# Where the scatters and transposes of a top-4-of-32 expert layer stand between the weight matmuls

## The chip, the core and the metric

The kernel runs on one NeuronCore of a Trainium2 chip. The metric is the device time of one execution in microseconds (us); the median of three runs of the kernel before is 1267.49 us (1266.92 to 1268.07). The engines are TensorE (PE, with its weight loads PEld), VectorE (DVE), ScalarE (ACT), GpSimd (POOL) and SyncE (SP), which issues the loads of the weights.

## The reference

One decoder layer on 512 tokens of 1024 numbers, all in float32: a mixing part (pooling and attention, not touched here) and then a mixture of 32 experts, of which each token takes four.

```
logits = ht @ w_router + b_router
top_vals, top_idx = lax.top_k(logits, TOP_K)
gates = jax.nn.softmax(top_vals, axis=-1)
...
gu = xblk @ w_gate_up[e] + b_gate_up[e]
gate = jnp.minimum(gu[:, :D_EXPERT], SWIGLU_LIMIT)
up = jnp.clip(gu[:, D_EXPERT:], -SWIGLU_LIMIT, SWIGLU_LIMIT)
act = gate * jax.nn.sigmoid(SWIGLU_ALPHA * gate) * (up + 1)
return act @ w_down[e] + b_down[e]
...
y = jnp.zeros((T + 1, D), h.dtype).at[row_tok].add(row_gate[:, None].astype(h.dtype) * yb)
```

After it the residual is added and a last RMSNorm is taken. Every expert's weights are read once, 12 MB each.

## The kernel before

The first 200 us hold the mixing part and the router. Then comes the loop that this change touches: 32 positions, each with one expert, ordered by how many tokens an expert has. `KINDS` says of a position whether it is small (S, up to 64 tokens) or big (B, up to 128).

A position has twelve **items**: eight of gate and up (`gu`, k = 0 to 7) and four of down (`dn`, j = 0 to 3), with 1 MB of weights each, which SP loads into a ring of slots. A big item splits its weights into a rounded part (`mhi`, by ACT, L937) and a rest (`mlo`, by DVE or POOL, L938), and multiplies three ways at full width: twelve matmuls into banks `x`. A small item multiplies in float32 with 64 columns of the array, two matmuls side by side, into banks `y`; each of its instructions shows as two rows in the profile. A planner (`interleave`) lays down once for all how the items of big positions (and of 0 and 31), called x, and those of the small ones, called y, take turns; its result `plan` is fixed and not touched. A row of small items in the plan without a big one in between is called a small block.

Around the items there is smaller work that PE also does, all of it through two PSUM banks `m`:

- `gather(r)`: two groups of four transposes that turn the rows fetched for a position (`xr`). For a big position four ACT pieces (`xgh`, L894) and four DVE pieces (`xgl`, L895) empty each group; for a small pair one DVE pass does (`xgs`, L917).
- `turn(r)`: transposes of the activation `au` (L1004 to L1008 compute it, from `ag` to `au`), emptied into `ats`, or `ath` and `atl`. There is a queue "turn x" for big positions and "turn y" for small ones.
- `arrive`: the slot sums, four short matmuls from `aux` and `oh`, and the fetch by an indirect DMA.
- `rest`: above all `combine`, the **scatter** of a finished position back to the tokens: eight times two matmuls at full width (`sc` with `ybh` and `ybl`, or `ss` with `ysh` and `ysl`), each pair followed by a DVE add into `y` (L1148).

Each of these is a generator in one of five queues, and `step` advances the first of every queue by one piece. Before, `step()` is called once behind every item, and in a big item once more in its middle (where `gate_up` and `down` yield). PE keeps the order in which the program writes it; on DVE and ACT a scheduler orders the work when the program is built. A piece of `turn` that is still waiting is taken in front of the down item that needs it.

Of the kernel before, what the change touches and what calls it, by code (L numbers as in the profile page):

```python
# [51 lines left out]
GAPX, GAPY, GAPN, GAPEND = 5, 2, 1, 3  # L52
TURN, SHORT = 0.2, 3.0
NFREE = 12
FILL1 = 2
FT = 3
FN = ((0, 1), (1, 3), (1, 3), (3, 4))
# [43 lines left out]
def mm3(pe, out, shi, slo, mhi, mlo, first, last):  # L101

    pe.matmul(out, lhsT=shi, rhs=mhi, start=first, stop=False)
    pe.matmul(out, lhsT=shi, rhs=mlo, start=False, stop=False)
    pe.matmul(out, lhsT=slo, rhs=mhi, start=False, stop=last)
# [20 lines left out]
def block_kernel(ctx: ExitStack, tc: tile.TileContext, xT, x, pos, vecs, w_in, w_pool, w_qb, w_kvb, w_out,  # L126
# [19 lines left out]
    y = cst.tile([P, NT, D], F32, name="y")  # L146
# [257 lines left out]
    for g, w in enumerate(WINDOWS):  # L404
        cur, step, lo_ = us[g], 1, 1
# [138 lines left out]
    def out_proj(z, c, tt):  # L544

        cs = slice(c * T, (c + 1) * T)
        for k in range(4):
            if ("out", z, c, k) in wraw:
                parts[z, c, k] = split_w(("out", z, c, k))
        po = {}  # L550
        for k in range(4):
            for t in tt:
                if k == 0:
                    po[t] = pt("po", bufs=5 if c and z else 7)
                ts = slice(t * P, (t + 1) * P)
                mm3(PE, po[t], mix["h", z][:, k, ts], mix["l", z][:, k, ts], *parts[z, c, k], k == 0, k == 3)
                yield
        for t in tt:
            V.scalar_tensor_tensor(y[:, t, cs], po[t], grms[z][:, t:t + 1], y[:, t, cs], op0=ALU.mult, op1=ALU.add)
# [193 lines left out]
    for t in range(NT):  # L753
        for _ in out_proj(1, 1, [t]):
            for _ in range(FILL1):
                while todo and next(todo[0], 0) == 0:
# [26 lines left out]
    def bank(tag):  # L783
        return pools["pm"].tile([P, T], F32, tag=tag, bufs={"x": 4, "y": 2, "m": 2}[tag], name=tag)
# [57 lines left out]
    onehot, slots, xg, yb, scat, actT = {}, {}, {}, {}, {}, {}  # L842

    def big(r):
        return r == "o" or KINDS[r] == "B"

    def onx(r):

        return big(r) or r == 0 or r == E - 1
# [94 lines left out]
    def split_item(r, what, k):  # L944

        w = wslots.pop((r, what, k))
        out_ = []
        for hf in range(2):
            out_.append(split(w[:, hf * D:(hf + 1) * D], G if nsplit[0] % 4 == 1 else V))
            nsplit[0] += 1  # L950
        presplit[r, what, k] = out_

    def fixed(r):
        return r != "o" and r < NFIX

    def biases(r, cs):
        for c in cs:
            bs = bias[:, c * T:(c + 1) * T]
            if big(r):
                PE.matmul(banks[r][c], lhsT=m4b[0:96, r:r + 1].to_broadcast([96, P]), rhs=bs, start=True, stop=False)  # L960
            else:
                q = 64 * (c % 2)
                PE.matmul(banks[r][c // 2][q:q + 64, :], lhsT=m4b[0:96, r:r + 1].to_broadcast([96, 64]), rhs=bs,
                          start=not fixed(r), stop=fixed(r))

    def gate_up(r, k):

        first = r == "o"
        if k == 0:
            banks[r] = [bank("x" if onx(r) else "y") for _ in range(4 if big(r) else 2)]  # L970
        if big(r):

            todo = [(hf, c) for hf in range(2) for c in range(2)] if k < KD - 1 else [
                (hf, c) for c in range(2) for hf in range(2)]
            parts = presplit.pop((r, "gu", k))
            for n, (hf, c) in enumerate(todo):
                cs = slice(c * T, (c + 1) * T)
                if k == 0 and not first:
                    biases(r, [2 * hf + c])
                mm3(PE, banks[r][2 * hf + c], xg[r][0][:, k, :], xg[r][1][:, k, :], parts[hf][0][:, cs],  # L980
                    parts[hf][1][:, cs], first and k == 0, k == KD - 1)
                if n == 1:
                    yield
        else:
            w = wslots.pop((r, "gu", k))
            for c in range(4):
                q = 64 * (c % 2)
                if k == 0 and c % 2 == 0 and not fixed(r):
                    biases(r, [c, c + 1])
                PE.matmul(banks[r][c // 2][q:q + 64, :], lhsT=xg[r][:, k, :], rhs=w[:, c * T:(c + 1) * T],  # L990
                          start=(k == 0 and fixed(r)), stop=(k == KD - 1 and not fixed(r)))

                if k == KD - 1 and c % 2 == 1 and fixed(r):
                    biases(r, [c - 1, c])
# [16 lines left out]
    def act(r):  # L1011
        b = banks.pop(r)
        return [swiglu(b[c], b[2 + c]) for c in range(2)] if big(r) else [swiglu(*b)]
# [139 lines left out]
    def spread(gf):  # L1153

        for c in range(2):
            cs = slice(c * T, (c + 1) * T)
            pb = bank("m")
            PE.matmul(pb, lhsT=ones[0:1, :], rhs=gf[0:1, cs], start=True, stop=True)
            S.copy(gf[:, cs], pb)
# [258 lines left out]
    plan = [v for b in blocks for v in b]  # L1418
# [13 lines left out]
    def later(g, n):  # L1432

        for _ in range(n):
            yield
        yield from g


    groups = {}
# [6 lines left out]
    def arrive(r):  # L1446

        for q in groups[r]:
            select(q)
            yield  # L1450
            slot_info(q)
        fetch(r)
# [3 lines left out]
    def load(what, r, k):  # L1456

        if r < NFIX and r not in wgu:
            wgu[r] = load_expert(r, r)
        if r not in wgu:  # L1460
            with tc.issue_after(lastload[-1]):
                wgu[r] = load_expert(r, nc.sync.value_load(eid[0:1, r:r + 1], min_val=0, max_val=E - 1))
        if what == "gu":
            load_gate_up(r, wgu[r], [k])
        elif r == E - 1:
            load_down_last(r, wdown[r], k)
        else:
            load_down(r, wdown[r], [k])
# [12 lines left out]
    def firsts(g):  # L1481
        return plan.index(("gu", g, 0))
# [4 lines left out]
    bigs = [r for r in range(E) if big(r)]  # L1487
# [6 lines left out]
            assert fetch_at[g] > KD, g  # L1494
    queues = {"turn x": [], "turn y": [], "gather": [], "arrive": [], "rest": []}

    def step(drain=None):

        for name, q in queues.items():
            if drain and name not in drain:  # L1500
                continue
            while q:
                if next(q[0], 0) == 0:
                    q.pop(0)
                elif not drain:
                    break
# [21 lines left out]
    for i, (what, r, k) in enumerate(plan):  # L1528

        PE.on = i >= NFREE  # L1530
        while loaded < min(i + (14 if i > 2 else 9), len(loads)):
            load(*loads[loaded])
            loaded += 1
        if big(r):
            n = xorder.index((what, r, k))
            assert n < nsp
        for g, at in fetch_at.items():
            if at == i:
                queues["arrive"].append(arrive(g))
        for g, at in turn_at.items():  # L1540
            if at == i:
                queues["gather"].append(gather(g))
        if (what, r, k) == ("gu", E - 1, 0):
            gf = mo.tile([P, D], F32, tag="xgh", bufs=1, name="gf")
            dma(gf[0:1, :], g_final)
        if k == 0 and what == "gu" and r > 0:
            assert r in xg, (r, i)
        if what == "dn" and k == 0:
            step(("turn x" if onx(r) else "turn y",))
        if what == "dn" and k == KD // 2 - 1:  # L1550

            while ("b" if big(r) else "s") in pending:
                step()
        if (what, r, k) == ("dn", E - 1, 0):
            step(queues)
            down_last(r, gf)
            break
        for _ in gate_up(r, k) if what == "gu" else down(r, k):
            step()

        ahead = n + 3 if big(r) else 2 if (what, r, k) == ("dn", 0, KD // 2 - 2) else 0
        for v in xorder[nsp:ahead]:
            split_item(v[1], v[0], v[2])
        nsp = max(nsp, min(ahead, len(xorder)))
        if what == "gu" and k == KD - 1:
            if r == E - 1:
                spread(gf)
            queues["turn x" if onx(r) else "turn y"].append(later(turn(r, act(r)), 3))
        if what == "dn" and k == KD // 2 - 1 and r < E - 2:
            if big(r):  # L1570
                queues["rest"].append(later(marked("b", combine([r])), 3))
            elif halfdone[0] is None:
                queues["rest"].append(later(marked("s", combine(["s"], r < NFIX)), 3))
        step()
    rt.close()

    PE.on = False
# [95 lines left out]
```

## Time and profile before

| what | value |
|---|---|
| median of three runs | 1267.49 us |
| profiled execution | 1268.17 us, span 1266.4 us |
| granted clock, mean over the span | 0.981 |
| PE busy | 1213.0 us (96%) |
| DVE busy | 865.4 us (68%) |
| ACT busy | 542.7 us (43%) |
| POOL busy | 303.7 us (24%) |
| HBM read | 429.71 MB, 343 GB/s over the span |
| chain that ended last | PE 74%, DVE 7% |

The span runs from the first to the last instruction of one profiled execution; 1.8 us lie around it. Busy shares are means over parts with different limits. A row of the timeline gives an instruction's start and length, and in brackets how long its engine stood idle before it and what ended that. PE rows overlap: the distance of two starts tells what one costs, not the length.

### The profile page before, as it was taken

Reading aid. Unit: us, or ns where it says so; the run is one execution under the profiler, and the core shown is the slowest. Engines: PE = TensorE matmul, PEld = TensorE weight load, DVE = VectorE, ACT = ScalarE, POOL = GpSimd, SP = SyncE. Lnnn points to the kernel's source line nnn. Section 1 sums busy time; section 2 is a strip of 40 time slices with the busy share of each in tenths; the row PEclk is TensorE's granted clock in tenths of the full one; section 3 lists DMA queues with packets and bytes.
Section 4 is the critical chain, followed back from the end, with each engine's and each line's share of the span. In section 5 each row is a group of like instructions: output and inputs, shape, how many; then the busy total and the mean of one; then the engine's idle time right before and its main releaser. Section 6 shows DMA issues by size and latency. Waiting matters only on the chain.

```text
span 1266.4 us, 16525 instructions
## 1 busy us (share of the span) xinstructions
PE 1213.0 (96%) x5597; PEld 697.3 (55%) x5597; DVE 865.4 (68%) x1552; ACT 542.7 (43%) x785; POOL 303.7 (24%) x272
## 2 busy tenths in 40 slices
PE   7979999899999998999999999999999999999994
PEld 6856674345655555555555555555645555555332
DVE  6897674657767676676768667776765876767344
ACT  6466650135525443354354435435434454444013
POOL 2355362112212121221123113221312122212001
PEclk9999999899999998999999999999999999999997
DMA  8312428999999998999998999999999999999981
GB/s 313 100 51 88 146 90 313 409 421 415 416 419 411 404 405 322 360 413 416 402 377 348 420 388 399 402 386 393 381 416 358 361 421 403 377 380 399 422 333 69
DMA packets 86849, 435.17 MB, mean 344 GB/s; under 512 B 9223, under 2 KB 9223, under 8 KB 53992
## 3 DMA queue, kind: packets, MB, share of 16 engines
q1 hardware_dynamic: 82818, 420.43, 83.4%
q0 software_dynamic: 3744, 13.24, 2.7%
q8 instruction: 45, 0.74, 0.2%
q10 hardware_dynamic: 198, 0.39, 0.1%
q14 instruction: 44, 0.36, 0.1%
HBM read 429.71 MB, written 4.33 MB: 343 GB/s over the span
## 4 chain that ended last, share of the span: by engine, by line
PE 74%; DVE 7%; DMA 1%; issue 1%; ACT 1%; POOL 0%; DVEq 0%; ACTq 0%; POOLq 0%
PE x L118 33%; PE y L118 29%; PE m L118 11%; DVE mlo L938 3%; DMA bdraw<-in_b_down_dram 1%; DVE au L1007 1%; ACT mhi L937 1%; DVE oh L859 0%; DVE au L1008 0%; DVE ag L1004 0%; DVE au L1006 0%; DVE xgl L895 0%; DVE ss L1096 0%; DVE y L1130 0%; DVE o L1186 0%
## 5 line engine op out<-in xcount | busy, mean ns | idle before, releaser
L937 ACT CAST mhi<-slot 128x1024 fp32r<-128x1024 f32 x288 | 300.6, 1049 | 260.9 <-PE x L118 236.1
L938 DVE TENSOR_TENSOR mlo<-slot,mhi 128x1024 fp32r<-128x1024 f32 x216 | 288.3, 1347 | 66.3 <-ACT mhi L937 65.8
L938 POOL TENSOR_TENSOR mlo<-slot,mhi 128x1024 fp32r<-128x1024 f32 x72 | 177.4, 2464 | 642.5 <-ACT mhi L937 642.4
L118 PE MATMUL y<-slot,xgs 128*64 128x512 f32 x1152 | 276.0, 602 | 0.0
L1148 DVE TENSOR_TENSOR y<-y,m 128x512 f32<-128x512 f32 x168 | 115.0, 684 | 121.8 <-PE m L118 121.4
L118 PE MATMUL x<-mhi,xgh 128*128 128x512 f32 x384 | 164.0, 427 | 0.0
L118 PE MATMUL x<-mlo,xgh 128*128 128x512 f32 x384 | 152.0, 396 | 0.1
L118 PE MATMUL x<-mhi,xgl 128*128 128x512 f32 x384 | 151.4, 394 | 0.0
L118 PEld LDWEIGHTS y<-slot,xgs 128*64 128x64 f32 x1152 | 76.1, 137 | 130.4 <-issue 126.9
L118 PE MATMUL y<-slot,ats 128*64 128x512 f32 x608 | 144.5, 612 | 0.7 <-ACT ats L1036 0.7
L1005 ACT ACTIVATE as<-ag 128x512 f32<-128x512 f32 x44 | 27.8, 632 | 160.7 <-DVE ag L1004 160.7
L118 PEld LDWEIGHTS x<-mhi,xgh 128*128 128x128 f32 x384 | 72.7, 189 | 25.7 <-issue 12.2
L118 PEld LDWEIGHTS x<-mhi,xgl 128*128 128x128 f32 x384 | 72.1, 188 | 17.0
L118 PEld LDWEIGHTS x<-mlo,xgh 128*128 128x128 f32 x384 | 72.4, 189 | 15.9 <-DVE mlo L938 1.1
L118 PEld LDWEIGHTS y<-slot,ats 128*64 128x64 f32 x608 | 39.7, 138 | 74.3 <-issue 70.5
L118 PE MATMUL x<-mhi,ath 128*128 128x512 f32 x192 | 64.2, 416 | 0.0
L118 PE MATMUL x<-mlo,ath 128*128 128x512 f32 x192 | 61.4, 401 | 0.0
L118 PE MATMUL x<-mhi,atl 128*128 128x512 f32 x192 | 60.9, 398 | 0.0
L1098 ACT ACTIVATE ysh<-y,sl 64x512 fp32r<-64x512 f32 x36 | 24.6, 684 | 80.4 <-PE y L118 80.1
L1100 DVE SCALAR_TENSOR_TENSOR ysl<-y,sl,ysh 64x512 fp32r<-64x512 f32 x36 | 27.0, 750 | 42.4 <-ACT ysh L1098 41.9
L881 POOL DMA_INDIRECT xr<-hrow,idx x21 | 28.7, 1367 | 94.5 <-DVE idx L878 48.7
L894 ACT ACTIVATE xgh<-m,gs 128x128 fp32r<-128x128 f32 x96 | 33.4, 366 | 31.9 <-PE m L118 16.7
(401 smaller groups left out, 1737.1 us busy)
## 6 DMA issues: line engine op xcount, KB each, us to landing
slot<-in_w_gate_up_dram SPq DMA_DIRECT2D x256, 1024.0 KB, 10.4
slot<-in_w_down_dram SPq DMA_DIRECT2D x128, 1024.0 KB, 9.9
wraw<-in_w_in_dram SPq DMA_DIRECT2D x16, 256.0 KB, 5.7
wraw<-in_w_out_dram SPq DMA_DIRECT2D x16, 256.0 KB, 2.6
xtraw<-in_xT_dram SPq DMA_DIRECT2D x8, 256.0 KB, 5.9
y<-in_x_dram SPq DMA_DIRECT2D x4, 512.0 KB, 7.3
hrow<-part POOLq DMA_DIRECT2D x8, 256.0 KB, 3.3
out_dram<-o SPq DMA_DIRECT2D x4, 512.0 KB, 2.7
```

Of the source, the lines that this page charges most:

```text
L118: r = f(*args, **kwargs)
L881: G.indirect_dma_start(out=rows[r], out_offset=None, in_=hrow, in_offset=bass.IndirectOffsetOnAxis(ap=idx[:, 0:1], axis=0), bounds_check=T ...
L894: S.activation(hi[:, d, :], v, AF.Copy, scale=g)
L937: S.copy(hi, src)
L938: eng.tensor_tensor(lo, src, hi.bitcast(F32), op=ALU.subtract)
L1005: S.activation(sg, g, AF.Sigmoid, scale=1.702)
L1007: V.scalar_tensor_tensor(u, u, 1.0, g, op0=ALU.add, op1=ALU.mult)
L1098: S.activation(yh[ps_, c], db[ps_, :], AF.Copy, scale=slots[r][ps_, 6:7])
L1100: V.scalar_tensor_tensor(yl[ps_, c], db[ps_, :], slots[r][ps_, 6:7], yh[ps_, c].bitcast(F32), op0=ALU.mult, op1=ALU.subtract)
L1148: V.tensor_tensor(y[:, t, cs], y[:, t, cs], pb, op=ALU.add)
```

## The change

`step` gets a second argument, `only`: the queues that may advance. With it:

- Behind a small item only "turn x" advances, but for the last item of a small block, behind which two full steps are taken.
- If a big position comes up within `SOON` = 4 items and its rows are not gathered yet, "gather" may advance behind a small item as well.
- In the middle of a big item every queue but `rest` advances, so no scatter stands there; behind it all do.
- Where a position's rows are still missing at its first item, the gather is driven until they are there.

```diff
+SOON = 4
...
-    def step(drain=None):
+    def step(drain=None, only=None):
 
         for name, q in queues.items():
-            if drain and name not in drain:
+            if name not in (drain or only or queues):
                 continue
...
         if k == 0 and what == "gu" and r > 0:
-            assert r in xg, (r, i)
+            while r not in xg:
+                step(only=("gather",))
...
+        beside = None if onx(r) or i < firsts(bigs[0]) else ("turn x",)
+        within = beside or ("turn x", "turn y", "gather", "arrive") if big(r) else beside
+        if beside and any(0 < firsts(g) - i <= SOON and g not in xg for g in groups if big(g)):
+            beside += ("gather",)
         for _ in gate_up(r, k) if what == "gu" else down(r, k):
-            step()
+            step(only=within)
...
-        step()
+        if beside and i + 1 < len(plan) and onx(plan[i + 1][1]):
+            for _ in range(2):
+                step()
+        else:
+            step(only=beside)
```

The plan of items, the loads and the arithmetic stay as they are. The order moves on PE, DVE and ACT; SP's is the same.

**PE, items 0 to 2 of gate and up of small position 9** (a small block between big position 6's items; `y` matmuls are the small ones, `sc` with `ybh` and `ybl` a scatter), before:

```order
L118 MATMUL y<-slot,xgs 64x512 x2
L118 MATMUL m<-ybh,sc 128x512
L118 MATMUL m<-ybl,sc 128x512
L118 MATMUL y<-slot,xgs 64x512 x4
L118 MATMUL m<-ybh,sc 128x512
L118 MATMUL m<-ybl,sc 128x512
L118 MATMUL y<-slot,xgs 64x512 x4
L118 MATMUL m<-ybh,sc 128x512
L118 MATMUL m<-ybl,sc 128x512
```

and now:

```order
L119 MATMUL y<-slot,xgs 64x512 x10
L119 MATMUL m<-ybh,sc 128x512
L119 MATMUL m<-ybl,sc 128x512
L119 MATMUL m<-ybh,sc 128x512
L119 MATMUL m<-ybl,sc 128x512
```

The three scatters that stood behind one item each are two at the block's end; the third has moved elsewhere.

**PE, item 7 of gate and up of small position 15, where the rows of big position 12 are gathered** (`m<-ident,xr` is a group of a gather, `ss` with `ysh` and `ysl` a scatter of a small pair, `x` the down items of big position 10), before:

```order
L118 MATMUL y<-slot,xgs 64x512 x4
L118 MATMUL m<-ident,xr 128x128 x4
L118 MATMUL x<-mhi,ath 128x512 x2
L118 MATMUL x<-mlo,ath 128x512 x2
L118 MATMUL x<-mhi,atl 128x512 x2
L118 MATMUL m<-ident,xr 128x128 x4
L118 MATMUL x<-mhi,ath 128x512 x2
```

and now:

```order
L119 MATMUL y<-slot,xgs 64x512 x4
L119 MATMUL m<-ident,xr 128x128 x4
L119 MATMUL m<-ysh,ss_4832 128x512
L119 MATMUL m<-ysl,ss_4832 128x512
L119 MATMUL m<-ident,xr 128x128 x4
L119 MATMUL m<-ysh,ss_4831 128x512
L119 MATMUL m<-ysl,ss_4831 128x512
L119 MATMUL x<-mhi,ath 128x512 x2
```

Both groups and two scatters now stand in one place, four writes of the two `m` banks in a row.

**DVE, from the gather of big position 14 to the scatters behind the last down item of big position 12** (`xgl` are the pieces that empty the gather, `ybl` closes the down product, `y<-y,m` is the add behind a scatter), before:

```order
L895 SCALAR_TENSOR_TENSOR xgl<-m,gs,xgh 128x128 x7
L1100 SCALAR_TENSOR_TENSOR ysl<-y,sl,ysh 64x512 x2
L895 SCALAR_TENSOR_TENSOR xgl<-m,gs,xgh 128x128
L938 TENSOR_TENSOR mlo<-slot,mhi 128x1024
L1148 TENSOR_TENSOR y<-y,m 128x512
L938 TENSOR_TENSOR mlo<-slot,mhi 128x1024
L1148 TENSOR_TENSOR y<-y,m 128x512
L1066 SCALAR_TENSOR_TENSOR ybl<-x,sl,ybh 128x512 x2
```

and now:

```order
L1101 SCALAR_TENSOR_TENSOR ysl<-y,sl,ysh 64x512 x2
L896 SCALAR_TENSOR_TENSOR xgl<-m,gs,xgh 128x128 x2
L939 TENSOR_TENSOR mlo<-slot,mhi 128x1024
L896 SCALAR_TENSOR_TENSOR xgl<-m,gs,xgh 128x128 x2
L939 TENSOR_TENSOR mlo<-slot,mhi 128x1024
L896 SCALAR_TENSOR_TENSOR xgl<-m,gs,xgh 128x128 x2
L1067 SCALAR_TENSOR_TENSOR ybl<-x,sl,ybh 128x512 x2
L939 TENSOR_TENSOR mlo<-slot,mhi 128x1024
L896 SCALAR_TENSOR_TENSOR xgl<-m,gs,xgh 128x128 x2
L1149 TENSOR_TENSOR y<-y,m 128x512 x3
```

The last two pieces of the gather stood ahead of `ybl` and now stand behind it and behind one more `mlo`.

## Rows read from the trace of the kernel before

**Rows 1.** The page's head: span, then busy time, share and instructions.
```profile
span 1266.4 us, 16525 instructions
PE 1213.0 (96%) x5597; PEld 697.3 (55%) x5597; DVE 865.4 (68%) x1552; ACT 542.7 (43%) x785; POOL 303.7 (24%) x272
```
**Rows 2.** Windows: length, busy by engine, granted clock, DMA share, GB/s.
```profile
300.00:400.00 100.00, 100.00 (x460) 56.87 (x457) 74.89 (x118) 44.43 (x56) 19.89 (x10) 1.00 1.02 416
```
**Rows 3.** Waits of PE, 240 to 1225 us: total, times, longest.
```profile
PE m L118 <- DVE xgl L895: 9.2, 4, 4.2
```
**Rows 4.** Waits of ACT for a DMA, same stretch.
```profile
ACT mhi L937 <- DMA slot<-in_w_gate_up_dram: 4.1, 1, 4.1
```
**Rows 5.** Chain that ended last, 449 to 456 us: start, length, what.
```profile
449.86 5.30 PE y L118 x24
```
**Rows 6.** Timeline of PE: start, length, what.
```profile
317.39 0.66 PE L118 MATMUL m<-ident,au 128*128 128x128 f32 x4
317.98 1.94 PE L118 MATMUL y<-slot,xgs 128*64 128x512 f32 x8
...
428.69 1.94 PE L118 MATMUL y<-slot,xgs 128*64 128x512 f32 x8
...
431.22 1.94 PE L118 MATMUL y<-slot,xgs 128*64 128x512 f32 x8
...
508.06 0.40 PE L118 MATMUL m<-ybh,sc 128*128 128x512 f32 x1
...
508.53 0.40 PE L118 MATMUL x<-mhi,xgh 128*128 128x512 f32 x1
```
**Rows 7.** Timeline of PE at the gather of big position 8.
```profile
475.56 0.60 PE L118 MATMUL m<-ident,xr 128*128 128x128 f32 x4
475.91 0.48 PE L118 MATMUL m<-ysh,ss 128*128 128x512 f32 x1
...
477.85 0.60 PE L118 MATMUL m<-ident,xr 128*128 128x128 f32 x4
...
482.69 0.79 PE L118 MATMUL m<-ysh,ss 128*128 128x512 f32 x1 [4.24 <-DVE xgl L895]
```
**Rows 8.** Groups by line, loop alone: count, busy us, mean ns, idle before.
```profile
L938 DVE TENSOR_TENSOR mlo<-slot,mhi 128x1024 fp32r<-128x1024 f32 x216 | 288.3, 1347 | 66.3 <-ACT mhi L937 65.8
L1148 DVE TENSOR_TENSOR y<-y,m 128x512 f32<-128x512 f32 x167 | 114.3, 684 | 121.8 <-PE m L118 121.4
...
L895 DVE SCALAR_TENSOR_TENSOR xgl<-m,gs,xgh 128x128 fp32r<-128x128 f32 x96 | 31.5, 345 | 21.0 <-ACT xgh L894 20.3
...
L1066 DVE SCALAR_TENSOR_TENSOR ybl<-x,sl,ybh 128x512 fp32r<-128x512 f32 x24 | 16.9, 738 | 1.3 <-ACT ybh L1065 1.3
...
L937 ACT CAST mhi<-slot 128x1024 fp32r<-128x1024 f32 x288 | 300.6, 1049 | 260.9 <-PE x L118 236.1 <-issue 15.9 <-DMA slot<-in_w_gate_up_dram 4.1
...
L1065 ACT ACTIVATE ybh<-x,sl 128x512 fp32r<-128x512 f32 x24 | 15.3, 685 | 7.4 <-PE x L118 7.1
```
**Rows 9.** Timeline of PE at the gathers of big positions 12 and 20.
```profile
637.48 0.66 PE L118 MATMUL m<-ident,xr 128*128 128x128 f32 x4
...
644.70 0.66 PE L118 MATMUL m<-ident,au 128*128 128x128 f32 x4 [1.96 <-DVE xgl L895]
...
941.40 0.66 PE L118 MATMUL m<-ident,xr 128*128 128x128 f32 x4 [2.70 <-DVE xgl L895]
```
**Rows 10.** Timeline of PE, then DVE, at the gather of big position 14.
```profile
713.52 0.66 PE L118 MATMUL m<-ident,xr 128*128 128x128 f32 x4
...
715.40 0.35 DVE L895 SCALAR_TENSOR_TENSOR xgl<-m,gs,xgh 128x128 fp32r<-128x128 f32 x1 [0.18 <-ACT xgh L894]
716.19 0.35 DVE L895 SCALAR_TENSOR_TENSOR xgl<-m,gs,xgh 128x128 fp32r<-128x128 f32 x1 [0.44 <-ACT xgh L894]
```
**Rows 11.** Windows behind the waits of rows 7 and 9.
```profile
482.00:489.00 7.00, 6.31 (x16) 4.96 (x17) 3.29 (x6) 1.66 (x3) 0.00 (x0) 0.54 0.95 392
...
645.00:649.00 4.00, 4.00 (x14) 2.16 (x14) 3.08 (x5) 3.71 (x7) 2.04 (x1) 0.57 0.59 211
```

## The prediction

> **What bounds the kernel now.** I read the page first: TensorE (PE) is busy 96% of the 1266.4 us span [rows 1]. Then the window table: where nothing stalls PE is busy 100 us of 100, and the weight stream, at 416 GB/s, fills its DMA share as well [rows 2]. Both are full, so I asked the waits which of them ends last. PE's largest wait in the loop is for VectorE (DVE), 9.2 us for the pieces `xgl` that empty a gather's transposes [rows 3]; for a weight slot ScalarE (ACT) waited once, 4.1 us [rows 4], and PE not at all. So the loop is bound by PE's own sequence plus its stalls, and each us off that sequence counts, up to the rate of the loads.
>
> **Part 1, fewer breaks in small blocks (gain).** Small experts' matmuls go in 64-column pairs (`128*64`), all else in full width (`128*128`). Three small items in one run take 5.30 us, 1.77 each [rows 5]; an item with a scatter behind it takes 431.22 - 428.69 = 2.53, so the scatter's pair costs 0.76 there, and inside a big item 508.53 - 508.06 = 0.47 [rows 6]. A break for a scatter thus costs 0.29 us beyond its work. Four transposes in a small block take 317.98 - 317.39 = 0.59 [rows 6], in a big item 475.91 - 475.56 = 0.35 [rows 7]: 0.24 beyond their work. In the printed order of the whole loop, other work than a big item's breaks a run of small items 86 times before and 29 times after: with a scatter in it 47 and 5 times, without one 39 and 24. Gain: 42 x 0.29 + 15 x 0.24 = 15.8 us; 13 to 18 as first matmuls after a switch vary. A scatter taken out of a big item's middle gains nothing, for it cost no switch there.
> The Trainium skill ("TensorEngine Tiling (Array Packing)", Tiling Modes, Key Properties) says that a change of tiling mode drains the engine, and "TensorE: Matmul & The Clock Gate" (Single matmul latency) puts a drain at about 175 ns; by that 57 breaks of two switches would be an estimated 20 us, and the sum 4 us lower. The trace's 0.29 per break is less than two such drains, and I go by it.
>
> **Part 2, what now stands behind a gather's second half (loss).** Scatters, transposes and slot sums all write the two `m` banks. For a big position a gather is two groups of four transposes, each emptied by four pairs of an ACT piece `xgh` and a DVE piece `xgl` of 0.345 [rows 8]. Whoever writes `m` next waits until the first group's last piece is out. The trace has three such waits: 4.24 us for a scatter right behind the second group [rows 7], 1.96 and 2.70 for transposes some us later [rows 9]. From the first group to the release it is 482.69 - 475.56 = 7.1 and 644.70 - 637.48 = 7.2 us. In the other gathers the next `m` write came too late to wait. The change delays scatters, so more of them stand right there. Place by place, from the order:
> - Big position 6 (down item 1): before, no scatter was left; now half an item, second group, scatter, as at 477.85. Emptying takes 3.0 us from the second group where ACT and DVE are free (713.52 to 716.54 [rows 10]) and 4.8 at 477.85 [rows 7]; less the group's own 0.35 the wait is 2.7 to 4.5, and I take 3.5, for DVE's order here has two `mlo` in between, as at 477.85, but PE holds less before it. Position 24: the same, 3.5. Position 8 had 4.24 and keeps it.
> - Position 12 (behind gate-up item 7 of small 15) and 18 (behind that of 23): group, scatter, group, scatter with nothing between. The second group needs the first scatter's bank, freed by a DVE add (0.684) that stands behind `ag`, `au`, `au` (of the same shape, taken at the same 0.684) and an `xgl`: 4 x 0.684 + 0.345 = 3.1 [rows 8] less 0.8 of PE work, about 2.4 with hand-over; the second scatter then waits for an `au` and for five pieces, three steps of 716.19 - 715.40 = 0.79 [rows 10] with a piece of each bank in a step, some 2.5 after its own group. Together 4.9 each (3.3 to 5.8). Position 12's 1.96 goes away for it: +2.9 and +4.9.
> - Position 14: both groups now stand at the block's end. DVE's order has the last two pieces behind `ybl`, `ybl` and a `mlo`, which need the end of down item 3; the scatter stands right behind that item. Serially: `ybh` 2 x 0.685, `mhi` 1.049, `mlo` 1.347, `xgl` 0.345 [rows 8] and hand-over: 4.4 us, with PE having nothing else. No wait before.
> - Position 16: a `mlo` now stands ahead of the last two pieces, for which its `mhi` waits for PE half an item earlier: 1.05 + 1.35 + 0.7 + 0.3 - 1.4 = 1.9 (0 to 2.5).
> - The 2.70 at 941 goes: three small items, 5.30 us [rows 5], stand in front of the next gather.
> Sum: 3.5 + 3.5 + 0 + 2.9 + 4.9 + 4.4 + 1.9 - 2.7 = +18.4 us (9 to 27). ACT and DVE are the cover that could hide it; it is gone, as they do this work in the order printed and PE holds no item ahead of the waiting one.
>
> **Part 3, the clock.** PE idled 4.24 and 1.96 us, and then the granted clock was 0.54 over 7 us and 0.57 over 4: most of these stretches at the lower level, 1.2 GHz [rows 11]. At half speed 7 x 0.46 = 3.2 and 4 x 0.43 = 1.7 us were lost; I take 2.2 for each, nearer the shorter. I now count seven waits of 1.9 us or more against three: +4 x 2.2 = 8.8 (4 to 13).
>
> **Part 4, short queues on the two banks.** Scatter, slot sum, scatter in a row (four block ends) hold PE for a DVE add of 0.68 less the work between, 0.8; group, scatter, group, scatter of small pairs (three) 0.9; two groups behind a transpose (one) 0.9; five scatters ahead of the last down item of small 26 and of 30 wait 0.3 to 0.4 for each add beyond the second, 1.2 each. 3.2 + 2.7 + 0.9 + 2.4 = 9.2; some 1 us of `au` and `xgs` waits of before goes. I take +8 (3 to 12). The transposes of a small activation come half an item earlier, about 3.4 us after the block; their chain is `ag` and three `au`, 2.8 us and hand-over: nothing on average. SP's order of loads is unchanged; the 15 us behind the loop keep their order.
>
> **Sum.** 1268.17 (profiled execution: span 1266.4 and 1.8 around it; 0.7 above the median of 1267.49) - 15.8 + 18.4 + 8.8 + 8 = 1287.6; set against the median 1286.9, so **1287 us**. Ends: 1267.5 - 18 + 9 + 4 + 3 = 1265.5 and 1267.5 - 13 + 27 + 13 + 12 = 1306.5, both unlikely together.
>
> **Rivals.**
> 1. Faster: the gathers empty fast. While PE stands, ACT gets no more `mhi` work, for that waits for PE (236.1 of 260.9 us [rows 8]), and the pieces come at 0.79 a step. For it: the gather at 713.52 [rows 10]. Against: at 475.56 it took 7.1 us with such a stall [rows 7]. If the first group is out within 2 us of the second (the point from which it decides), the waits sum to some 13 us against 8.9, the clock drops are two instead of three (-2), the short queues cost 3, and the gain of 17 wins: 1267.5 + 4 - 2 + 3 - 17 = 1256.
> 2. No change: the loads set the pace. For it: a DMA share of 1.02 where nothing stalls [rows 2]. Then a wait of PE only fills slots that PE later empties, and saved switches only run into the loads: 1268. Against: one wait for a slot in the loop [rows 4].
> 3. Worse: every long wait brings the drop after the 4.24 one, 3.2 us [rows 11], and takes the upper price: 1303.
> That the change does not do what it says is excluded by the order, which shows the breaks gone.
> The Trainium skill ("TensorEngine Tiling (Array Packing)", Performance Considerations, PSUM Bottleneck) warns that emptying PSUM may become the bound once the matmuls are packed; the waits [rows 7, 9] show that here at three places alone, and I let it price only the places named above.
>
> **How the numbers follow.** Forecast 0.60, faster rival 0.18, no change 0.10, worse 0.12. A measurement tells 0.2% (2.5 us) from no change. Faster 0.18, same 0.10, slower 0.72. The range leaves out most of the faster rival and the far end of the worse one: 1262 to 1304.
>
> **What would show it.** In the trace after: `PE m <- DVE xgl` some 27 us instead of 9.2, at seven places; as many slices with a lower granted clock; and small runs of 5 to 7 us unbroken. Wrong if `xgl` waits stay below 12 us, or if PE starts to wait for weight slots.

## The result and the profile after

The changed kernel takes 1289.24 us (1288.82 to 1294.38), the kernel before 1267.78 us (1266.92 to 1268.07) beside it: a ratio of 1.0181, 95% interval 1.0163 to 1.0199. It is 21.5 us slower; the prediction was 1287.

The profiled execution is the longest of the four, 1294.38 us. Its page's head answers to [rows 1]:

```profile
span 1292.7 us, 16508 instructions
PE 1208.8 (94%) x5597; PEld 709.8 (55%) x5597; DVE 864.2 (67%) x1552; ACT 543.4 (42%) x785; POOL 302.3 (23%) x272
```

PE does the same 5597 matmuls in a longer span. Where it stands idle in the loop is told by the waits of PE, 240 to 1225 us (total, times, longest), the answer to [rows 3]:

```profile
PE m L119 <- DVE xgl L896: 23.7, 7, 5.2
PE m L119 <- DVE y L1149: 7.8, 8, 2.6
PE m L119 <- DVE xgs L918: 3.6, 5, 1.9
PE m L119 <- DVE au L1009: 1.5, 3, 0.7
PE y L119 <- DVE ysl L1101: 1.2, 1, 1.2
PE x L119 <- DVE mlo L939: 0.6, 1, 0.6
PE m L119 <- DVE atl L1034: 0.6, 1, 0.6
PE m L119 <- DVE sl L930: 0.5, 1, 0.5
```

Almost all are waits of writes of the two `m` banks. (L119 is a helper's line, which every matmul has; the banks tell them apart.) PE still waits for no weight slot, and ACT's only wait for a transfer there has shrunk from 4.1 us [rows 4] to 1.4:

```profile
ACT mhi L938 <- DMA slot<-in_w_gate_up_dram: 1.4, 1, 1.4
```

**Where the waits are.** The timeline of PE at the gather of big position 12 (start, length, what, in brackets the idle time before and what ended it):

```profile
644.73 0.66 PE L119 MATMUL m<-ident,xr 128*128 128x128 f32 x4
645.14 0.48 PE L119 MATMUL m<-ysh,ss 128*128 128x512 f32 x1
645.46 0.40 PE L119 MATMUL m<-ysl,ss 128*128 128x512 f32 x1
648.49 1.03 PE L119 MATMUL m<-ident,xr 128*128 128x128 f32 x4 [2.63 <-DVE y L1149]
651.40 0.79 PE L119 MATMUL m<-ysh,ss 128*128 128x512 f32 x1 [1.89 <-DVE xgl L896]
```

Group, scatter, group, scatter, with 4.5 us of standing in them. Position 18 has the same with 1.32 and 1.89. The one long wait each at positions 6, 8, 16 and 24:

```profile
411.33 0.80 PE L119 MATMUL m<-ysh,ss 128*128 128x512 f32 x1 [4.05 <-DVE xgl L896]
...
494.52 0.50 PE L119 MATMUL m<-ysh,ss 128*128 128x512 f32 x1 [4.57 <-DVE xgl L896]
...
817.89 0.24 PE L119 MATMUL m<-aux,oh 128*128 128x4 f16 x4 [2.84 <-DVE xgl L896]
...
1120.69 0.79 PE L119 MATMUL m<-ysh,ss 128*128 128x512 f32 x1 [3.24 <-DVE xgl L896]
```

At position 14 it is one wait too; first the scatter behind down item 3 of position 12 on PE, then DVE in the same stretch:

```profile
727.89 1.10 PE L119 MATMUL m<-ident,xr 128*128 128x128 f32 x8
...
739.75 0.79 PE L119 MATMUL m<-ysh,ss 128*128 128x512 f32 x1 [5.20 <-DVE xgl L896]
```

```profile
734.34 2.13 DVE L939 TENSOR_TENSOR mlo<-slot,mhi 128x1024 fp32r<-128x1024 f32 x1 [1.09 <-ACT mhi L938]
736.39 0.60 DVE L896 SCALAR_TENSOR_TENSOR xgl<-m,gs,xgh 128x128 fp32r<-128x128 f32 x2
736.91 1.39 DVE L1067 SCALAR_TENSOR_TENSOR ybl<-x,sl,ybh 128x512 fp32r<-128x512 f32 x2
738.23 1.21 DVE L939 TENSOR_TENSOR mlo<-slot,mhi 128x1024 fp32r<-128x1024 f32 x1
739.36 0.59 DVE L896 SCALAR_TENSOR_TENSOR xgl<-m,gs,xgh 128x128 fp32r<-128x128 f32 x2
```

The last pieces stand behind `ybl` and an `mlo`, as the printed order had it, and PE starts 0.2 us before they end by the records.

**The lower clock.** In 240 to 1225 us there were three such stretches before and there are seven now. Windows of the changed kernel (length, busy time of PE, PEld, DVE, ACT, POOL, then granted clock, DMA share, GB/s):

```profile
409.70:416.50 6.80, 5.17 (x12) 4.11 (x13) 2.49 (x8) 2.44 (x6) 0.00 (x0) 0.50 1.03 423
...
737.40:744.20 6.80, 4.45 (x12) 1.61 (x14) 3.24 (x6) 0.04 (x1) 0.00 (x0) 0.50 1.01 418
...
sum 37.50, PE 30.17 PEld 19.99 DVE 18.37 ACT 7.00 POOL 1.23; mean PE 4.31 PEld 2.86 DVE 2.62 ACT 1.00 POOL 0.17
```

and the sum of the three of before:

```profile
sum 13.60, PE 12.61 PEld 7.41 DVE 6.51 ACT 5.07 POOL 1.54; mean PE 4.20 PEld 2.47 DVE 2.17 ACT 1.69 POOL 0.51
```

At 0.50, which is 1.2 GHz, I count half of PE's busy time as lost: 15.1 us against 6.3. (The expectations below still reckon with 16.4 and 5.5 us.)

**Time that is not the change's.** 5.7 us of this execution's extra length lie ahead of the first item of big position 2 (269 us in the kernel before), where the order is the old one. PE waited there once for a count of the router; the waits of PE, 205 to 240 us, have this row, and the kernel before has none like it:

```profile
PE x L119 <- DVE nblk L1329: 4.3, 1, 4.3
```

The wait comes and goes between traces: that of the kernel before with a hold (below) has it, that of the changed kernel with the hold has not. The changed kernel's other three runs are 5.1 to 5.6 us shorter. Traces of the experiments begin the loop 0.4 to 5.7 us later than that of before; where I say "loop" below, this start is taken off.

**The account.** The span grew by 26.3 us, 20.6 without that start. Waits for `xgl`, with the two adds at 12 and 18 that belong to them: 23.7 + 2.6 + 1.3 - 9.2 = +18.4. Lower clock: +8.8. Short waits (adds 3.9, `xgs` 3.6, `au` 1.5, `mlo` 0.6, `atl` 0.6, `sl` 0.5, less 2.2 of before): +8.5. Together +35.7; what the breaks gave back is the rest, 35.7 - 20.6 = 15.1 us. It is a remainder here; the experiments measure it in other ways.

### The profile page after: what moved, and what is told of

It reads as the page before. It is cut to its first block, busy times and chain, and to the rows that moved or that the text cites. A ratio compares the mean times of both kernels' runs of the same rounds, so it can differ in the third digit from the quotient of the medians.

```text
span 1292.7 us, 16508 instructions
## 1 busy us (share of the span) xinstructions
PE 1208.8 (94%) x5597; PEld 709.8 (55%) x5597; DVE 864.2 (67%) x1552; ACT 543.4 (42%) x785; POOL 302.3 (23%) x272
## 4 chain that ended last, share of the span: by engine, by line
PE 73%; DVE 8%; ACT 1%; DMA 1%; issue 1%; POOL 0%; ACTq 0%; DVEq 0%; POOLq 0%
PE x L119 33%; PE y L119 29%; PE m L119 10%; DVE mlo L939 2%; DMA bdraw<-in_b_down_dram 1%; ACT mhi L938 1%; DVE oh L860 1%; DVE y L1149 1%; DVE xgl L896 1%; DVE au L1008 0%; DVE au L1007 0%; ACT xgh L895 0%; DVE xgs L918 0%; DVE ag L1005 0%; DVE ysl L1101 0%
## 5 line engine op out<-in xcount | busy, mean ns | idle before, releaser
L119 PE MATMUL y<-slot,xgs 128*64 128x512 f32 x1152 | 271.4, 605 | 0.0
L119 PE MATMUL x<-mhi,xgh 128*128 128x512 f32 x384 | 162.8, 424 | 0.0
L119 PEld LDWEIGHTS y<-slot,xgs 128*64 128x64 f32 x1152 | 79.9, 138 | 141.4 <-issue 138.8
L119 PE MATMUL x<-mlo,xgh 128*128 128x512 f32 x384 | 152.3, 397 | 0.7 <-DVE mlo L939 0.6
L119 PE MATMUL x<-mhi,xgl 128*128 128x512 f32 x384 | 151.5, 395 | 0.0
L119 PE MATMUL y<-slot,ats 128*64 128x512 f32 x608 | 136.6, 597 | 0.0
L119 PEld LDWEIGHTS y<-slot,ats 128*64 128x64 f32 x608 | 41.1, 137 | 79.6 <-issue 78.1
L119 PEld LDWEIGHTS x<-mlo,xgh 128*128 128x128 f32 x384 | 72.7, 189 | 17.2 <-DVE mlo L939 1.6
L119 PEld LDWEIGHTS x<-mhi,xgl 128*128 128x128 f32 x384 | 72.4, 188 | 17.2
L119 PEld LDWEIGHTS x<-mhi,xgh 128*128 128x128 f32 x384 | 73.0, 190 | 16.0 <-issue 1.6
L119 PE MATMUL x<-mhi,ath 128*128 128x512 f32 x192 | 65.2, 422 | 0.0
L119 PE MATMUL x<-mlo,ath 128*128 128x512 f32 x192 | 62.9, 410 | 0.0
L119 PE MATMUL x<-mhi,atl 128*128 128x512 f32 x192 | 62.0, 405 | 0.0
L119 PE MATMUL m<-ysh,ss 128*128 128x512 f32 x72 | 33.0, 458 | 22.2 <-DVE xgl L896 20.8
L119 PE MATMUL m<-ybh,sc 128*128 128x512 f32 x96 | 42.5, 443 | 5.6 <-DVE y L1149 3.7
```

The source lines that it names most:

```text
L119: r = f(*args, **kwargs)
```

## The experiments

**Keeping the scatters away from the gathers.** The first theory was that a scatter, moved away, finds the bank free. The first line stands in `gather` behind each group of a big position, the others in `step`; `now[0]` is the item's index in the plan. An item that cannot go on without a scatter lifts the hold.

```diff
+                now[1] = now[0] + 2
...
+            if not drain and name != "gather" and now[0] + ("turn" in name) < now[1]:
+                continue
```

> The changed kernel, in which a big position's gather, once a group of it is issued, keeps scatters and slot sums back until two items of the plan later (transposes of activations until one item later). My theory: the loss is PE standing behind the pieces xgl (23.7 us in the changed kernel's trace, and 3.9 us more for an add of a scatter between two groups at positions 12 and 18) and the lower clock behind these waits (10.9 us more than before). Six of the seven waits go; that at position 16 stays and may grow, since the scatters held there are then forced ahead of the last down item. Minus 25 of waits, minus 10 of clock, plus 3 for bursts of scatters elsewhere: 1257 us (1250 to 1265). Rival, the loads set the pace: the waits go but PE waits for weight slots instead, 1280 or more. Rival, the loss is in the bursts of short work on the two m banks: these stay, so 1280 or more, with the xgl waits gone.

> The kernel before with the same hold and nothing of the change. My theory: its waits behind the gathers of positions 8 and 12 (4.2 and 2.0 us) and the two stretches of lower clock behind them (3.2 and 1.7) go; the 2.7 at 941 us, where the next gather itself waits, stays. 1267.8 - 6.2 - 4.9 = 1257 us (1254 to 1262). It then stands level with the changed kernel with the hold, because that one has 16 us less of breaks, 8 more of short queues and one wait left of some 5 with its lower clock. Rival, the waits are free since the loads set the pace: 1267.

Measured: 1288.88 us (1285.07 to 1289.89; ratio 1.0160, 1.0137 to 1.0182) and 1272.9 us (1.0040, 1.0024 to 1.0056). Both expectations fell, by 32 and 16 us. But neither rival of the first explains it, for both take the waits to be gone, and they hardly shrank: 20.7 us of 23.7, again seven. Waits of PE, changed kernel with the hold:

```profile
PE m L119 <- DVE xgl L896: 20.7, 7, 4.7
PE m L119 <- DVE y L1150: 6.9, 9, 1.7
```

The writers came later, and so did the pieces. DVE at the gather of position 8 with the hold, whose first group is at 478.59:

```profile
481.99 0.34 DVE L896 SCALAR_TENSOR_TENSOR xgl<-m,gs,xgh 128x128 fp32r<-128x128 f32 x1
482.25 1.21 DVE L940 TENSOR_TENSOR mlo<-slot,mhi 128x1024 fp32r<-128x1024 f32 x1
483.38 0.60 DVE L896 SCALAR_TENSOR_TENSOR xgl<-m,gs,xgh 128x128 fp32r<-128x128 f32 x2
483.90 1.21 DVE L940 TENSOR_TENSOR mlo<-slot,mhi 128x1024 fp32r<-128x1024 f32 x1
485.03 0.60 DVE L896 SCALAR_TENSOR_TENSOR xgl<-m,gs,xgh 128x128 fp32r<-128x128 f32 x2
486.36 2.48 DVE L940 TENSOR_TENSOR mlo<-slot,mhi 128x1024 fp32r<-128x1024 f32 x1 [0.73 <-ACT mhi L939]
488.77 0.60 DVE L896 SCALAR_TENSOR_TENSOR xgl<-m,gs,xgh 128x128 fp32r<-128x128 f32 x2
```

In the changed kernel the first group was out 7.0 us after its start; here it takes 489.4 - 478.6 = 10.8, for three `mlo` now stand between these pieces, where there was one in the changed kernel. An `mlo` needs an `mhi`, and that waits for PE to go on (236.1 of the 260.9 us that ACT stood before `mhi` in the kernel before [rows 8]). So the emptying has no length of its own: it is strung along PE's progress, and whoever writes `m` early stands until DVE has worked through what is queued. (The order of DVE is made at build time, so a hold on PE's side changes it too.) In the kernel before with the hold, 7.9 us of `xgl` waits stayed, and a new 3.8 us for `ats` came, at an activation's transposes that the hold had moved next to their use; its profiled loop was 1.3 us longer than that of before.

**The two halves alone.** Small items alone: `within = beside` for big items too (`None` there, so in their middle every queue advances, as before). Big items alone: `beside = None`, so all queues advance behind every item.

> The half of the change that concerns the small items alone: scatters and transposes stand at the end of a small block; in a big item's middle every queue advances, as before. My theory, from the printed order: the gain of breaks is whole (-15.8); xgl waits at positions 8 (4.2), 12 and 18 (3.5 each, an activation's transposes behind two groups in a row), 14 (3) and 16 (2.5), none at 6 and 24: 17 us against 9.2, two more drops of the clock (+4.4), short queues +5. Sum +1.5: 1269 us (1262 to 1276). Rival, the two halves simply add up and each costs about half: 1278.

> The half of the change that concerns big items alone: no scatter in their middle; behind every item, small ones too, all queues advance one piece. My theory, from the printed order: 101 breaks of small runs instead of 86 (+4.5), the wait at position 8 goes (-4.2 and its lower clock -3.2), one at 24 comes (+3.5 and +2.2), short queues +1: 1267.8 + 3.8 = 1271.6 us (1266 to 1276). So the two halves give +5 and the whole change +21: the rest comes from both together, that is from scatters which find no other place than right behind a gather. Rival, the halves add up: 1278.

Measured: 1270.53 us (1.0020, 1.0011 to 1.0030) and 1279.18 us (1.0091, 1.0074 to 1.0108). The small half is as expected, with 15.5 us of `xgl` waits at five places for 17. By its loop (0.6 us longer than that of before), its waits (15.0 us more) and its lower clock (1.7 more) the breaks gave 16 us there. The big half is 7.6 us above the expectation and outside its range. Its profiled loop is only 5.8 us longer than that of before, for 3.8 expected, with 10.4 us of `xgl` waits for 8.5 expected, and 4.8 us of its time lie ahead of the loop. The other three runs have a mean granted clock of 0.980 where the profiled one has 0.986, at the same time; where they spent it isn't recorded, so this miss stays open in part. The halves together make 2.6 + 11.3 = 13.9 us by the medians, the whole change 21.5 (6.4 and 20.6 by the profiled loops): 8 to 14 us arise only from both; by the printed order these are scatters that have lost one place and are put into bursts at the other.

**Emptying the bank faster.** If the length of the emptying is the cause, PE's order may stay as it is. One DVE pass takes a group out of the bank, and the split is made from the copy:

```diff
-                for i in range(4):
-                    split_rows(4 * b + i, v[:, i, :])
+                gsl = slice(4 * b, 4 * b + 4)
+                xt = mo.tile([P, T], F32, tag="as" if b else "ag", bufs=1, name="xgt")
+                xt = xt.rearrange("p (a b) -> p a b", b=P)
+                V.tensor_tensor(xt, v, gs[:, gsl].unsqueeze(2).to_broadcast([P, 4, P]), op=ALU.mult)
+                S.copy(hi[:, gsl, :], xt)
+                V.tensor_tensor(lo[:, gsl, :], xt, hi[:, gsl, :].bitcast(F32), op=ALU.subtract)
```

> The changed kernel with its order on TensorE untouched, but a big position's gather is emptied another way: one DVE pass per group (128x512, times the gains) takes the transposes out of the bank m, and the split into xgh and xgl is made from that copy in SBUF. The bank is then free behind one pass instead of four pairs of pieces, and in the printed order of DVE at most one mlo stands ahead of that pass. My theory, the loss is PE standing behind the slow emptying, and the lower clock behind it: of 23.7 us of xgl waits some 3 stay, of the 16.4 us lost at the lower clock some 6 (those behind other waits): 1289.2 - 20 - 10 = 1259 us (1252 to 1267). Rival, the loads set the pace: PE waits for weight slots instead, 1280 or more. Rival, the bursts of short work on the two banks are the loss: they stay, 1280 or more. The hold of the scatters gave nothing, 1288.9, and with it the waits stayed at 20.7: my theory says because the pieces too left later, so this run has to bring what that one did not.

> The kernel before with the same emptying. My theory: of its 8.9 us of xgl waits at three places some 1 stays, and of 5.5 us at the lower clock some 1: 1267.9 - 12 = 1256 us (1252 to 1262). The changed kernel with this emptying then has 16 us less of breaks and 8 us of short queues, and 5 us more of lower clock behind those: level with it within 8 us. Rival, loads set the pace: 1267.

> The half of the change for small items alone, with the same emptying. Without it the half cost 2.6 us against the kernel before: breaks -16, xgl waits 15.5 against 9.2, lower clock 7.3 against 5.5, short waits (au, adds, xgs) 11 against 2.5. My theory: the xgl waits fall to 2 and the lower clock to 4, so 1270.5 - 13.5 - 3.3 = 1254 us (1249 to 1260), the fastest of the three. Rival, the gain of breaks isn't there and the waits alone made the difference: level with the kernel before in its own faster emptying, or above it by the 8 us of short waits.

Measured: 1255.81 us (ratio 0.9907, 0.9890 to 0.9923), 1256.58 us (0.9914, 0.9897 to 0.9930) and 1245.79 us (0.9823, 0.9806 to 0.9839). Waits of PE of the whole change with this emptying:

```profile
PE m L119 <- DVE y L1149: 7.5, 9, 2.4
PE m L119 <- DVE xgs L918: 3.6, 5, 1.9
PE m L119 <- DVE xgt L914: 2.3, 3, 1.0
PE m L119 <- DVE au L1009: 1.5, 3, 0.7
```

The row of 23.7 us is one of 2.3, the short waits are nearly all still there, and of the lower clock two stretches of 3.4 us are left, so some 3.5 us lost instead of 15.1. That is 21.4 + 11.6 = 33.0 of the 33.4 us gained. PE's order is untouched, so the `xgl` waits with the clock behind them are what made the change slower; the bursts, which are still there, don't make it so alone, and the loads don't set the pace. The kernel before lost its `xgl` row altogether, and with it 11.2 us (1256 expected). The small half came out 8 us below its expectation and 3 below its range. Against the same half without this emptying, its waits fell by 14.3 us (27.6 to 13.3) and its loss at the lower clock by some 6.3; 3 to 4 us of the gain are not accounted for.

Two more things follow from the three. First, breaks: the small half with the faster emptying stands 10.8 us under the kernel before with it (10.5 by the loops), though its trace has 6.8 us more of waits (12.1 against 5.3, without `ysl`, which both have) and as much time at the lower clock; so the breaks gave some 17 us, if none of those 3 to 4 us belongs elsewhere. Second, the big half costs 10.0 us even so, of which the rows show 6 (waits 17.5 against 13.3, lower clock 3.5 against 1.7): at position 12, for example, the burst still stands 2.39 and 0.64 us, with an add and an `xgt` as releasers.

**Three more edits, and the price of one break.** The two groups of a big activation's transposes in one place and one item later, and the scatter ahead of the slot sum in a step:

```diff
-            if c:
-                yield
             tp = bank("m")
...
+        yield
...
-    queues = {"turn x": [], "turn y": [], "gather": [], "arrive": [], "rest": []}
+    queues = {"turn x": [], "turn y": [], "gather": [], "rest": [], "arrive": []}
...
-            queues["turn x" if onx(r) else "turn y"].append(later(turn(r, act(r)), 3))
+            queues["turn x" if onx(r) else "turn y"].append(later(turn(r, act(r)), 4 if big(r) else 3))
```

> The half for small items with the faster emptying, and three more edits: both groups of a big activation's transposes stand in one place and one item later; in a step the scatter goes ahead of the slot sum. It tests the price of a break by itself: 12 places of the order fewer at which a run of small items is broken for transposes, 0.24 us each by the prediction's rows, 2.9 us. Beside it the two waits of 2.3 us for au go (4.5), and of six waits of 0.7 for a scatter's add behind a slot sum 0.4 each (2.4). My theory: 1245.8 - 9.8 = 1236 us (1233 to 1242). Rival: breaks cost nothing beyond their work, so only the waits count: 1239. Rival: the transposes in one place wait for the second activation or for the emptying, or the loads now set the pace: 1244 or more.

> The whole change with the faster emptying and the same three edits as in the run beside it. It differs from that one by the big items alone: no scatter in their middle. My theory: these scatters then stand in bursts (group, scatter, group, scatter at positions 12 and 18, five in a row ahead of the last down items of small 26 and of 30), which cost 10.0 us between the two runs without these edits (1255.8 against 1245.8). So it stands 7 to 11 us above the run beside it: 1245 us (1241 to 1250). Rival: the bursts are not the cause and the difference came from one state of the run: within 2 us of it.

Measured: 1249.59 us (0.9859, 0.9842 to 0.9877) and 1252.78 us (0.9878, 0.9858 to 0.9899). Both lie outside their ranges. The first missed by 13.6 us and is slower than without the edits (1245.79). The price of a break, though, can be read cleanly. PE in gate and up of small position 13, first without and then with the edits:

```profile
541.70 0.41 PE L119 MATMUL y<-bias,m4b 96*64 96x512 bf16 x2
...
543.02 4.46 PE L119 MATMUL y<-slot,xgs 128*64 128x512 f32 x20
547.41 0.66 PE L119 MATMUL m<-ident,au 128*128 128x128 f32 x4
548.00 1.94 PE L119 MATMUL y<-slot,xgs 128*64 128x512 f32 x8
549.87 0.66 PE L119 MATMUL m<-ident,au 128*128 128x128 f32 x4
550.45 1.08 PE L119 MATMUL y<-slot,xgs 128*64 128x512 f32 x4
```

```profile
543.67 0.41 PE L119 MATMUL y<-bias,m4b 96*64 96x512 bf16 x2
...
544.99 6.18 PE L119 MATMUL y<-slot,xgs 128*64 128x512 f32 x28
551.10 1.09 PE L119 MATMUL m<-ident,au 128*128 128x128 f32 x8
552.12 1.08 PE L119 MATMUL y<-slot,xgs 128*64 128x512 f32 x4
```

The same four items and eight transposes take 8.75 and 8.45 us: 0.30 for the one break less, and six other undisturbed places give 0.30 as well. Half of it stands ahead of the transposes: 28 small matmul rows in one run take 6.11 us, 20 and 8 take 4.39 + 1.87 = 6.26; the other half is in the transposes, 2 x 0.59 against 1.02. The edits' 3 us from this were lost. Little of that went into the waits, whose sum only grew from 13.3 to 15.2 us, but they stand elsewhere:

```profile
PE m L119 <- DVE au L1009: 4.0, 4, 1.5
PE m L119 <- DVE atl L1032: 2.7, 1, 2.7
```

Both groups in one place fill both banks, so the next writer waits for the emptying (2.7), or the second group waits for the second `au` (1.46, twice). Four stretches at the lower clock go with these waits, 13.39 us of PE at 0.50, 6.7 us lost, where the run without the edits had none up to 1200 us; they took back the gain. The fourth stands behind a wait for `ysl` that grew from 1.2 to 1.9 us. The whole change with the edits is 3.2 us above, not 7 to 11: it escaped the long `au` waits, so this pair does not isolate the big half.

**A version that keeps them apart.** The transposes stay in two places, and come an item later only where the block has five items:

```diff
-            queues["turn x" if onx(r) else "turn y"].append(later(turn(r, act(r)), 3))
+            queues["turn x" if onx(r) else "turn y"].append(later(turn(r, act(r)), 4 if i + 5 < len(plan) and not any(onx(v[1]) for v in plan[i + 1:i + 6]) else 3))
```

> The half for small items with the faster emptying; a big activation's transposes come one item later only where the small block has room for five items, and stay in two places; in a step the scatter goes ahead of the slot sum. From the run that had them in one place: at seven undisturbed places a break for transposes less gave 0.29 us (4.85 to 4.56 over two items), but waits for atl (2.7), au (1.46 twice) and ath (1.1) came, with 5 us more at the lower clock. Here the two groups keep an item between them, so these waits stay away and two au waits of 0.55 are left of two of 2.3. Ten breaks: -2.9; au: -3.4; adds behind slot sums: -1.8: 1245.8 - 8 = 1238 us (1236 to 1243). Rival: the order of DVE shifts again and a new wait of some us with its lower clock takes it back: 1244 to 1250.

Measured: 1238.96 us (1238.26 to 1240.84), ratio 0.9774, 0.9758 to 0.9790, for 1238 expected. Ten breaks less (3.0 us) and waits of 9.3 us for 13.3 make up the 6.8 us by which it stands under the small half with the faster emptying. It beats both kernels: 28 us under the kernel before and 50 under the changed one. Its window of 270 to 1200 us, beneath that of the changed kernel:

```profile
270.00:1200.00 930.00, 890.29 (x4030) 520.50 (x4027) 642.47 (x958) 402.70 (x507) 199.82 (x90) 0.98 0.96 384
```

```profile
270.00:1200.00 930.00, 920.74 (x4252) 533.17 (x4252) 667.49 (x936) 392.40 (x447) 205.38 (x90) 1.00 1.00 406
```

The loads followed at 406 GB/s instead of 384, and PE waited for no slot (ACT twice, 2.4 us in all): the pace of the slower kernels was not theirs. With a DMA share of 1.00 in this window, how much further they would follow is not shown.

## Why the prediction was right, point by point

- **Part 1, the breaks: right.** 15.8 us were predicted; the account leaves 15.1, the small half 16, and the pair with the faster emptying some 17. A break for transposes costs 0.30 us, not 0.24, so that term was 0.9 us short: its row begins at the transposes and leaves out what the small matmuls ahead of them lose. The price for a scatter, 0.29, was not measured by itself. The estimate of 0.35 per break and 20 us from the Trainium skill's drains ("TensorEngine Tiling (Array Packing)", Tiling Modes, Key Properties, with the 175 ns of "TensorE: Matmul & The Clock Gate", Single matmul latency) is too high; the runs are on the side of the row.
- **Part 2, the waits: right in sum, and place by place within 1.7 us.** That +18.4 came to the decimal is luck, since misses of up to 1.7 us cancel. Positions 6, 8, 12, 14, 16, 18, 24 were to stand 3.5, 4.2, 4.9, 4.4, 1.9, 4.9, 3.5 us, 27.3 together; they stood 4.05, 4.57, 4.52, 5.20, 2.84, 3.21, 3.24, together 27.6. The 2.70 at 941 us [rows 9] went. At position 16 the terms written down make 2.0, not 1.9. The largest miss is position 18: the scatter's add came 1.3 us after PE was ready, not 2.4, and the second scatter waited 1.9, not 2.5. The prediction took 3.0 to 4.8 us for the emptying, place by place from the printed order of DVE, and that held as long as the order was the printed one; it does not say that the emptying has no length of its own. The hold was reckoned as if it had one, and failed.
- **Part 3, the clock: right to the decimal, which is luck.** +8.8 was predicted and +8.8 came, 2.15 us for each stretch against 2.2 taken. But the pairing of waits and drops was not what I assumed: 1.32 and 1.89 us at position 18 had no drop behind them, and a drop at 856.8 us fell into a wait of 1.9 for `xgs`.
- **Part 4, short queues: right in sum.** +8 predicted, +8.5 in the account. In its parts it is less so: the adds brought 3.9 us where the block ends and the rows of five scatters were to bring 5.6, and 1.7 us for `mlo`, `atl` and `sl` were not in it.
- **The tells.** Some 27 us at seven places: 23.7 at seven by that row, the rest under the adds. "As many slices with a lower clock" holds. Unbroken small runs are there, `y` x24 of 5.37 us at 461.68 for example. PE waited for no slot.
- **The rivals.** The faster one asked for a first group out within 2 us of the second and named 1256. In the change as it was, the first group was out 5 us behind the second at position 8 (494.52 - 489.35), so its condition did not hold; the faster emptying brought it about, and the change then stood at 1255.8. Loads that set the pace are excluded by the 406 GB/s. The worse one named 1303 without its sum, from 3.2 us for each drop: the seven drops lost 1.5 to 2.9 us each.

## What to carry over

Before work is moved behind a step, ask how long the step's output bank stays full and whose order decides that. Here eight small pieces on two engines, strung between other work, held a bank for 7 us and more, and moving the writer only moved the pieces; one pass that copies the bank out was worth 33 us. A regrouping that saves switches pays once the banks turn round fast: with it the same small half went from 2.6 us lost to 10.8 gained. And two edits can cost more together (21.5 us) than their costs added up (13.9), if each takes away the place the other pushes work to.

## What the hardware showed that was not expected

- Breaking a run of 64-column matmuls for full-width transposes costs 0.30 us beyond their work, the same at seven places to 0.01.
- A wait of about 2 us is followed by the lower clock at one time and not at another: two of 2.27 us for `au` in the small half with the faster emptying had none behind them, and of the same two waits of 2.27 us in the small half without it the first (396 us) had none behind it and the second (626 us) had one; while 0.55 and 1.46 us with one group of transposes between them had one twice in the run with the three edits.
- The faster emptying makes DVE pass over every element twice, a copy and a subtraction, and costs it only 7.0 us in the loop: 96 pieces of 0.344 us (30.5 us) became 24 copies of 0.686 and 24 subtractions of 0.902 (37.5 us). ACT's part went from 31.9 to 14.7 us. Over the whole span DVE's busy time went from 864.2 to 871.3 us, ACT's from 543.4 to 530.1.
